# Neighbourhood attention of an encoder block: query products of 512 columns, and keys kept in token order

## The chip, the cores and the metric

The kernel runs on one core of a Trainium2 chip. The metric is the device time of one execution in microseconds (us); each kernel is run several times and the median is given. A profile is one more execution, recorded by the hardware profiler; its span runs from the first to the last instruction. Engines are named as the profile names them: PE (matrix products) with PEld (its weight loads), DVE (vector), ACT (scalar), POOL (GpSimd) and SP, which issues the DMAs.

## The reference, cut to what matters

One encoder block is computed for one sequence of 1024 tokens with 1024 features. After a modulated norm, one input projection gives queries, keys and values for two attentions, eight heads of 64 features each, and two gates. The change touches the second attention: the tokens stand on a grid of 16 rows and 64 columns, and each query attends to a window of 8 x 16 tokens that is clamped to the grid.

```python
q5 = q.reshape(B, rows, GRID_W, H, Dh)            # rows = 16, GRID_W = 64
row_start = jnp.clip(r - kh // 2, 0, rows - kh)   # kh = 8
col_start = jnp.clip(cq - NA_COLS // 2, 0, GRID_W - NA_COLS)   # NA_COLS = 16
s = jnp.einsum('brqhd,brakhd->bhrqak', q5, kr) * scale + bias[None]
s = jnp.where(col_mask[:, None, :], s, -jnp.inf)
p = jax.nn.softmax(s, axis=(-2, -1))
o = jnp.einsum('bhrqak,brakhd->brqhd', p, vr)
```

The first attention is a mixture of three dilated windows over the same sequence. Both outputs are projected, gated, summed, projected again and added to the residual; a ConvFFN (two large products with a depthwise convolution and a GELU between) and a final norm follow.

## The kernel before, in words

**Token order.** Everything is kept transposed, features on the 128 partitions and tokens along the free axis. The 1024 tokens stand in the order (r, t): position 256 r + t holds token 4 t + r. For the grid, t is 16 w + x, where w is the grid row and 4 x + r the grid column. So the order is (r, w, x): four residues, sixteen rows, sixteen groups of four columns. A half `hf` is the 512 positions with r = 2 hf and 2 hf + 1.

**Precision.** A product is made of three: each operand is split into a high part (rounded to fp32r) and a low part, and `product` (lines 78 to 85) issues high x high (L83), high x low (L84) and low x high (L85) for each of eight blocks of 128 features, into one PSUM bank of 512 columns. Weight tiles are loaded by SP (L64), rounded by ACT (L56), and POOL forms the low part (L60).

**Queries and keys of one pair of heads** (`qk_steps`, L284). For each of two halves a product goes into a bank `pj`; there are two such banks, `ps_g`, shared by queries, keys and gates. `q_half` (L291) empties the bank for each of the two heads: ACT writes the high part into `qs` (L305), DVE the difference (L306). `k_half` (L327) does the same with a factor 1/8: ACT L339, DVE L340, ACT L341, and POOL L342 copies the low part to the other 64 partitions.

**The neighbourhood branch (br = 1) before.** Its queries are wanted in the order (c, w, r, x'): c is one of four blocks of 16 columns, x' one of four groups in it, so that 128 neighbouring queries (one c, eight rows) form a block. `q_windows` (L308) therefore reads the moving operand `h` in that order, one residue at a time: for each of the eight blocks and three parts, two products of 256 columns (L315), 48 for a half instead of 24. The bank is then written to `qs` in runs of eight (L303 to L306). Its keys are stored in the order (w, x, r), so L339 to L342 write every fourth element of a half's share.

**The attention itself** (`attend_na`, L713). For each head, four blocks of columns `cb` and two row groups R: the score product (L735) takes 128 queries against twelve rows and n = 6 or 8 groups of columns, 288 or 384 keys, once with the high keys and once with the low ones; the keys of one row are one run of 24 or 32 elements. DVE adds the bias and takes the extreme (L739), ACT exponentiates (L741), DVE and POOL normalise (L746), PE transposes (L756), ACT and DVE split (L759, L760), PE multiplies with the values (L768), ACT and DVE add the two halves into the output tile (L774, L775), and SP writes it to `o_scr` (L776). The banks of the scores are two (`ps_l`).

**Values.** They are written to DRAM in token order and copied once per column block from DRAM to DRAM by 16 DMAs (`vb_chunks`, L382 to L387), into rows ordered like the keys: (w, x, r). `vb_load` (L539) loads them for each head.

**What sets the order.** The start (L389 to L537) and the gated branch products (L848 to L904) are written out by hand. Between them a scheduler orders the instructions of every engine by a timeline of its own: the loop at L790 issues, for eight pairs of heads (four dilated, four neighbourhood), the attention of pair n and then the queries and keys of pair n + 1 and one or two gates (`gate_tile`, L778). So products for the next pair fill PE while DVE and ACT work on scores. Gates evict through ACT L784. After the last gate the branch products need the last pair's output back from DRAM: `o_operands` (L822) loads it (L829), and ACT and DVE split it (L56, L60 into `o1hi`, `o1lo`). Then come the output projection and the ConvFFN (L906 on), again ordered by the scheduler.

Of the kernel before, what the change touches and what calls it, by code (L numbers as in the profile page):

```python
# [11 lines left out]
AF = mybir.ActivationFunctionType  # L12
OP = mybir.AluOpType
# [5 lines left out]
KT = 8  # L19
# [5 lines left out]
NA_T0 = (0, 2, 6, 10)  # L25
# [3 lines left out]
def hybrid_encoder(tc, xT, c, w_ada, small, w_in, p1_bias, p23_bias, na_bias, ln2_mult, ident, w_br, w_out,  # L29
                   w_up, w_down, out):  # L30
    nc = tc.nc
    act, dve, pool, pe, sp = nc.scalar, nc.vector, nc.gpsimd, nc.tensor, nc.sync
# [5 lines left out]
    def f(ap):  # L38
        return ap.bitcast(FT)
# [50 lines left out]
    h = {}  # L90
# [143 lines left out]
    vb_s = [v_scr[64 * sum(NA_NC[:cb]):64 * sum(NA_NC[:cb + 1])] for cb in range(4)]  # L234
# [49 lines left out]
    def qk_steps(br, pr, ws=None, ps=None):  # L284
        qt, kt = ((0, 4), (12, 16))[br]
        qs = [qkpool.tile([128, S], FR, name="qs") for _ in range(2)]
        ks = [qkpool.tile([128, S], FR, name="ks") for _ in range(2)]
        kl = [qkpool.tile([128, S], FR, name="kl") for _ in range(2)]
        qb = []

        def q_half(hf, w, p=None):  # L291
            cols = halves[hf]
            if p is None:
                p = ps_g.tile([128, 512], FT, name="pj")
                if br == 0:
                    product(p, w, lambda k: h[hf, k])
                else:
                    q_windows(p, w, hf)
            for i in range(2):
                a, b = slice(64 * i, 64 * i + 64), slice(64 - 64 * i, 128 - 64 * i)  # L300
                d, pp = qs[i][:, cols], p
                if br:
                    d = qs[i].rearrange("p (v r t) -> p v r t", v=64, r=4)[:, :, 2 * hf:2 * hf + 2]  # L303
                    pp = p.rearrange("p (r v t) -> p v r t", r=2, v=64)
                act.activation(d[a], pp[a], AF.Copy)  # L305
                dve.tensor_tensor(d[b], pp[a], f(d[a]), OP.subtract)  # L306

        def q_windows(p, w, hf):  # L308

            whi, wlo = w  # L310
            for k in range(KT):
                mhi, mlo = (t.rearrange("p (r w c t) -> p r c w t", r=2, w=16, c=4) for t in h[hf, k])
                for x, (ww, m) in enumerate(((whi, mhi), (whi, mlo), (wlo, mhi))):
                    for r in range(2):
                        pe.matmul(p[:, 256 * r:256 * r + 256], ww[:, k], m[:, r], start=k + x + r == 0,  # L315
                                  stop=k == KT - 1 and x == 2, skip_group_check=True)

        def q_blocks():
            for i in range(2):
                q = qkpool.tile([128, S], FR, name="qb", bufs=2)  # L320
                for r in range(4):
                    pool.tensor_scalar(q.rearrange("p (b r j) -> p r b j", b=8, r=4)[:, r],
                                       f(qs[i][:, 256 * r:256 * r + 256]).rearrange("p (b j) -> p b j", b=8), 1.0, None,
                                       OP.mult)
                qb.append(q)

        def k_half(hf, w, p=None):  # L327
            cols = halves[hf]
            if p is None:
                p = ps_g.tile([128, 512], FT, name="pj")  # L330
                product(p, w, lambda k: h[hf, k])
            for i in range(2):
                a, b = slice(64 * i, 64 * i + 64), slice(64 - 64 * i, 128 - 64 * i)
                kh, ll, pp = ks[i][:, cols], kl[i][:, cols], p
                if br:
                    kh, ll = (t.rearrange("p (w t r) -> p r w t", w=16, t=16)[:, 2 * hf:2 * hf + 2]
                              for t in (ks[i], kl[i]))
                    pp = p.rearrange("p (r w t) -> p r w t", r=2, w=16)
                act.activation(kh[a], pp[a], AF.Copy, scale=0.125)  # L339
                dve.scalar_tensor_tensor(ll[a], pp[a], 0.125, f(kh[a]), OP.mult, OP.subtract)  # L340
                act.activation(kh[b], pp[a], AF.Copy, scale=0.125)  # L341
                pool.tensor_scalar(ll[b], f(ll[a]), 1.0, None, OP.mult)  # L342

        if ws:
            for hf in range(2):
                yield
                if hf:
                    ps = [ps_g.tile([128, 512], FT, name="pj") for _ in range(2)]
                    for k in range(KT):
                        for p, w in zip(ps, ws):  # L350
                            product(p, w, lambda k: h[1, k], ks=[k])
                q_half(hf, ws[0], ps[0])
                k_half(hf, ws[1], ps[1])
            yield
            q_blocks()
        else:
            w = weights(qt + pr, pool)
            for hf in range(2):
                q_half(hf, w)
            if br == 0:  # L360
                q_blocks()
            w = weights(kt + pr, pool)
            for hf in range(2):
                k_half(hf, w)
        return qs, ks, kl, qb
# [16 lines left out]
    def vb_chunks():  # L382
        for cb in range(4):
            t0, n = NA_T0[cb], NA_NC[cb]
            for r in range(4):
                sp.dma_start(vb_s[cb].rearrange("(w t r) n -> r w t n", r=4, t=n)[r],
                             vb_c[256 * r:256 * r + 256].rearrange("(w t) n -> w t n", t=16)[:, t0:t0 + n])  # L387

    with tc.manual_schedule(engines={e.engine for e in (sp, act, dve, pool, pe)}):  # L389
        x = [x_load(0)]  # L390
# [34 lines left out]
        for q in range(4):  # L425
            ks = range(2 * q, 2 * q + 2)
# [76 lines left out]
        for n, (br, hv, st) in enumerate(v_steps[:19]):  # L503
# [17 lines left out]
            p = v_product(st, v_w[br, hv])  # L521
# [191 lines left out]
    def attend_na(pr, qk, work):  # L713
        qs, ks, kl, qb = qk
        oT = work.tile([128, S], FT, name="u1")
        for i in range(2):
            head = 2 * pr + i
            a = slice(64 * i, 64 * i + 64)
            kv, lv = (t.rearrange("p (w c) -> p w c", w=16) for t in (ks[i], kl[i]))
            st = work.tile([128, 2, 8], FT, name="stb")  # L720
            vv = v_tile(v_raw(vb_load, head), ((96, slice(0, 4)), (128, slice(4, 12)), (96, slice(12, 16))))
            col = 0
# [1 line left out]
            for cb in range(4):  # L724
                t0, n = NA_T0[cb], NA_NC[cb]
                kn = 48 * n
                bt = sm_pool.tile([128, 896], FT, name="bias", bufs=2)
                sp.dma_start(bt[:, :2 * kn], na_bias[head][:, col:col + 2 * kn])
                P = sm_pool.tile([128, 2, 384], FT, name="P", bufs=5)
                for R in range(2):  # L730
                    s = ps_l.tile([128, 512], FT, name="S")
                    d = s[:, :kn]
                    qc = slice(256 * cb + 128 * R, 256 * cb + 128 * R + 128)
                    for x_, t in enumerate((kv, lv)):
                        pe.matmul(d, qs[i][:, qc], t[:, 4 * R:4 * R + 12, 4 * t0:4 * t0 + 4 * n], start=x_ == 0,  # L735
                                  stop=x_ == 1)
                    e = 2 * cb + R
                    pp = P[:, R, :kn]
                    dve.tensor_tensor_reduce(pp, d, bt[:, kn * R:kn * R + kn], -1.0, BIG, OP.add, OP.min,  # L739
                                             st[:, 0, e:e + 1])  # L740
                    act.activation(pp, pp, AF.Exp, bias=st[:, 0, e:e + 1], scale=-1.0, accum_out=st[:, 1, e:e + 1])  # L741
                col += 2 * kn
                dve.reciprocal(st[:, 1, 2 * cb:2 * cb + 2], st[:, 1, 2 * cb:2 * cb + 2])  # L743
                for R in range(2):
                    pp = P[:, R, :kn]
                    (pool, dve)[R].tensor_scalar(pp, pp, st[:, 1, 2 * cb + R:2 * cb + R + 1], None, OP.mult)  # L746
                pn[cb] = P
            for pair in ((0, 3), (1, 2)):
                m = 16 * NA_NC[pair[0]]
# [13 lines left out]
                for y, cb in enumerate(pair):  # L763
                    jobs = ((1, t3[y], 128, 0, 256), (2, t3[2], 256 * y, 0, 256), (0, t3[y], 0, 0, 128),
                            (3, t3[y], 384, 128, 128))
                    for x_, (g, tt, c0, d0, n) in enumerate(jobs):
                        for t in tt:
                            pe.matmul(po[:, 256 * y + d0:256 * y + d0 + n], vv[:m, 4 * cb + g], t[:m, c0:c0 + n],  # L768
                                      start=x_ == 0 and t is tt[0], stop=x_ == 3 and t is tt[1],
                                      skip_group_check=True)  # L770
# [65 lines left out]
    with tc.tile_pool(name="gate", bufs=1, reuse_waits="tile") as work:  # L836
# [37 lines left out]
        for i in range(2 * KT):  # L874
            m, hf = divmod(i, 2)
            cols = halves[hf]
# [551 lines left out]
def _na_index():  # L1428
    parts = []
    p = np.arange(128)[:, None]  # L1430
    for cb in range(4):
        n = NA_NC[cb]
        for R in range(2):
            k = np.arange(48 * n)[None, :]
            qr, qc = 8 * R + p // 16, 16 * cb + 4 * (p % 4) + p // 4 % 4
            kr, kc = 4 * R + k // (4 * n), 4 * NA_T0[cb] + k % (4 * n)
            r0, c0 = np.clip(qr - 4, 0, 8), np.clip(qc - 8, 0, 48)
            ok = (kr >= r0) & (kr < r0 + 8) & (kc >= c0) & (kc < c0 + 16)
            idx = np.clip(kr - qr + 7, 0, 14) * 31 + np.clip(kc - qc, -15, 15) + 15
            parts.append(np.where(ok, idx, 15 * 31))  # L1440
    return np.concatenate(parts, axis=1)
# [58 lines left out]
```

## Time and profile before

| what | value |
|---|---|
| time, median of 3 runs | 1553.82 us |
| lowest and highest run | 1552.45 and 1553.98 us |
| span of the profiled execution | 1553.3 us, which lies between the lowest and the highest run |
| mean granted TensorE clock | 0.987 |
| instructions | 22335 |
| moved by DMA | 196.88 MB, mean 127 GB/s |

The profiled execution has no time of its own besides its span; the median of the timed runs stands 0.5 us above that span. The page gives for each engine its busy time and its share of the span. A matmul's duration on the page (some 280 ns for 256 columns, 390 ns for 512) is longer than the distance from one matmul's start to the next one's, because they are pipelined; what a product costs PE is read from starts. The branch named above runs from about 380 us (the first queries of a neighbourhood pair) to 684 us.

### The profile page before, as it was taken

How to read it: one execution, taken by the hardware profiler on the slowest of the kernel's cores; microseconds unless marked ns; L12 is line 12 of the kernel's file. 1: busy time of each engine (PE TensorE's matmuls, PEld its weight loads, DVE VectorE, ACT ScalarE, POOL GpSimd, SP SyncE). 2: the span in 40 equal slices, each digit the busy share in tenths (PEclk: the TensorE clock that was granted, in tenths of full speed). 3: DMA queues.
4: the chain of work that ended last, by engine and by line, in shares of the span. 5: the costliest groups of instructions: out<-in, count | busy, mean ns of one | idle time of the engine just before them, and what ended most of it. 6: DMA issues, size and time to landing. Idle time of an engine off the chain costs nothing.

```text
span 1553.3 us, 22335 instructions
## 1 busy us (share of the span) xinstructions
PE 1504.7 (97%) x8028; PEld 1291.5 (83%) x8028; DVE 1007.7 (65%) x1880; ACT 804.0 (52%) x1448; POOL 822.5 (53%) x652
## 2 busy tenths in 40 slices
PE   8998999999999999999999898999999998999998
PEld 7998988888898998878888777888888887878777
DVE  6785375665666665535615898766666667787765
ACT  4432475665866777543335454444444446575542
POOL 1043253544427666311256758776666665779721
PEclk9999999999999999999999999999999999999999
DMA  9467321222524443557734212222222224523313
GB/s 352 168 214 258 87 86 62 85 74 91 160 89 120 133 142 111 169 191 243 227 133 149 82 46 104 92 85 82 81 82 82 81 75 155 199 81 122 115 55 109
DMA packets 112374, 196.88 MB, mean 127 GB/s; under 512 B 39944, under 2 KB 57736, under 8 KB 112264
## 3 DMA queue, kind: packets, MB, share of 16 engines
q1 hardware_dynamic: 111992, 195.20, 38.1%
q8 instruction: 63, 1.03, 0.3%
q14 instruction: 47, 0.39, 0.1%
q10 hardware_dynamic: 272, 0.26, 0.1%
HBM read 158.73 MB, written 42.47 MB: 130 GB/s over the span
## 4 chain that ended last, share of the span: by engine, by line
PE 73%; DVE 8%; POOL 6%; DMA 5%; ACT 4%; issue 3%; SPq 1%; DVEq 0%; ACTq 0%; POOLq 0%
PE pj L83 11%; PE pj L84 11%; PE pj L85 10%; PE pj L963 8%; PE pj L965 8%; PE pj L964 8%; POOL wsl L60 2%; DMA wraw<-w_down 2%; PE pj L315 2%; PE O L768 2%; PE pv L243 2%; PE pv L245 1%; PE pv L244 1%; DVE big L1158 1%; PE T L756 1%
## 5 line engine op out<-in xcount | busy, mean ns | idle before, releaser
L60 POOL TENSOR_TENSOR wlo<-wraw,whi 128x512 fp32r<-128x512 f32 (+1 forms) x154 | 193.9, 1281 | 244.3 <-ACT whi L56 224.1
L83 PE MATMUL pj<-h,whi 128*128 128x512 f32 x448 | 179.2, 400 | 4.1 <-ACT ks L341 1.7
L84 PE MATMUL pj<-h,whi 128*128 128x512 f32 x448 | 177.9, 397 | 1.6 <-DVE h L208 1.6
L85 PE MATMUL pj<-h,wlo 128*128 128x512 f32 x448 | 176.9, 395 | 0.0
L60 POOL TENSOR_TENSOR wsl<-big,wsh 128x512 fp32r<-128x512 f32 (+1 forms) x90 | 123.8, 1397 | 51.8 <-ACT wsh L56 51.8
L56 ACT ACTIVATE whi<-wraw 128x1024 fp32r<-128x1024 f32 (+2 forms) x81 | 81.3, 1004 | 84.7 <-PE pj L84 36.3
L342 POOL TENSOR_SCALAR kl<-kl 64x512 fp32r<-64x512 f32 x32 | 63.8, 1995 | 99.2 <-DVE kl L340 97.9
L1158 DVE SCALAR_TENSOR_TENSOR big<-wc,sm,big 128x256 f32<-128x256 f32 (+1 forms) x132 | 103.0, 828 | 16.8 <-ACT big L1152 16.6
L83 PEld LDWEIGHTS pj<-h,whi 128*128 128x128 f32 x448 | 84.8, 189 | 20.3 <-ACT ks L341 2.5
L84 PEld LDWEIGHTS pj<-h,whi 128*128 128x128 f32 x448 | 84.8, 189 | 17.9 <-DVE h L208 3.1
L593 DVE CUSTOM_DVE_ANT_0 P<-S,bias 128x256 f32<-128x256 f32 x128 | 51.6, 420 | 73.6 <-PE S L640 47.0
L85 PEld LDWEIGHTS pj<-h,wlo 128*128 128x128 f32 x448 | 84.7, 189 | 15.6
L594 ACT ACTIVATE P<-P,st 128x256 f32<-128x256 f32 x128 | 64.2, 502 | 32.9 <-DVE st L593 32.3
L243 PE MATMUL pv<-vwh,h 128*128 128x256 f32 x256 | 74.7, 292 | 4.3 <-ACT vs L250 4.3
L60 POOL TENSOR_TENSOR wsl<-wraw,wsh 128x384 fp32r<-128x384 f32 (+1 forms) x46 | 54.7, 1212 | 44.5 <-ACT wsh L56 44.4
L1158 DVE SCALAR_TENSOR_TENSOR big<-pj,sm,big 128x512 f32<-128x512 f32 x132 | 67.1, 563 | 16.4 <-ACT big L1152 16.4
L1152 ACT ACTIVATE big<-wc,sm 128x512 f32<-128x512 f32 x44 | 35.8, 815 | 74.4 <-DVE wc L976 42.8
L550 POOL TENSOR_TENSOR vv<-vv 96x256 fp32r<-96x256 f32 (+2 forms) x32 | 41.1, 1292 | 62.7 <-ACT vv L549 42.8
L245 PE MATMUL pv<-vwh,h 128*128 128x256 f32 x256 | 73.7, 288 | 0.0
L244 PE MATMUL pv<-vwl,h 128*128 128x256 f32 x256 | 73.7, 288 | 0.0
L746 POOL TENSOR_SCALAR P<-P,stb 128x288 f32<-128x288 f32 (+1 forms) x32 | 39.4, 1233 | 47.9 <-DVE stb L743 38.9
L56 ACT ACTIVATE wsh<-big 128x1024 fp32r<-128x1024 f32 (+1 forms) x45 | 44.7, 998 | 38.2 <-POOL big L928 22.5
(380 smaller groups left out, 4885.1 us busy)
## 6 DMA issues: line engine op xcount, KB each, us to landing
wraw<-w_in SPq DMA_DIRECT2D x36, 512.0 KB
wada<-w_ada SPq DMA_DIRECT2D x31, 512.0 KB
big<-w_up SPq DMA_DIRECT2D x22, 512.0 KB
wraw<-w_up SPq DMA_DIRECT2D x22, 512.0 KB
as<-big SPq DMA_DIRECT2D x22, 512.0 KB
big<-as SPq DMA_DIRECT2D x22, 512.0 KB
wraw<-w_down SPq DMA_DIRECT2D x24, 384.0 KB
gs<-gs SPq DMA_DIRECT2D x32, 256.0 KB
```

The costliest lines, as they stand in the source:

```text
L56: act.activation(hi, raw, AF.Copy)
L60: lo_eng.tensor_tensor(lo[:, i:i + step], raw[:, i:i + step], f(hi)[:, i:i + step], OP.subtract)
L83: pe.matmul(psum, whi[:, k0 + k], mhi, start=k == 0, stop=False)
L84: pe.matmul(psum, whi[:, k0 + k], mlo, start=False, stop=False)
L85: pe.matmul(psum, wlo[:, k0 + k], mhi, start=False, stop=k == n - 1)
L243: pe.matmul(p, hhi, hi[:, k], start=fresh and k == 0, stop=False, skip_group_check=True)
L244: pe.matmul(p, hhi, lo[:, k], start=False, stop=False, skip_group_check=True)
L245: pe.matmul(p, hlo, hi[:, k], start=False, stop=k == KT - 1, skip_group_check=True)
L963: pe.matmul(psum, whi[:, k], bhi, start=j < 4 and k == 0, stop=False, skip_group_check=True)
L964: pe.matmul(psum, whi[:, k], blo, start=False, stop=False, skip_group_check=True)
L965: pe.matmul(psum, wlo[:, k], bhi, start=False, stop=k == n - 1, skip_group_check=True)
L1158: dve.scalar_tensor_tensor(y[:, dst], src, wt, y[:, dst], OP.mult, OP.add)
```

## The change

The query product of the neighbourhood branch is issued by `product`, 512 columns at a time. It reads `h` as (w, x, r): four neighbouring groups x of one residue, then the other residue of the half. The bank is written to `qs` in the same places as before, with another rearrangement. The keys stay in token order (r, w, x): the writes of L339 to L342 are plain. The score product's moving operand picks, for each of twelve rows and each of four residues, the n groups of columns it needs, so a run is 6 or 8 elements where it was 24 or 32. The bias (built on the host, `_na_index`) and the values (`vb_chunks`) take the same key order: row, residue, group. The DMAs from DRAM to DRAM then write n rows of 2 KB in one run.

```diff
             if br:
-                d = qs[i].rearrange("p (v r t) -> p v r t", v=64, r=4)[:, :, 2 * hf:2 * hf + 2]
-                pp = p.rearrange("p (r v t) -> p v r t", r=2, v=64)
+                d = qs[i].rearrange("p (c w x) -> p c w x", c=4, w=16)[:, :, :, 8 * hf:8 * hf + 8]
+                pp = p.rearrange("p (w c x) -> p c w x", w=16, c=4)
             act.activation(d[a], pp[a], AF.Copy)
             dve.tensor_tensor(d[b], pp[a], f(d[a]), OP.subtract)
...
         def q_windows(p, w, hf):
-            whi, wlo = w
-            for k in range(KT):
-                mhi, mlo = (t.rearrange("p (r w c t) -> p r c w t", r=2, w=16, c=4) for t in h[hf, k])
-                for x, (ww, m) in enumerate(((whi, mhi), (whi, mlo), (wlo, mhi))):
-                    for r in range(2):
-                        pe.matmul(p[:, 256 * r:256 * r + 256], ww[:, k], m[:, r], start=k + x + r == 0,
-                                  stop=k == KT - 1 and x == 2, skip_group_check=True)
+            product(p, w, lambda k: [t.rearrange("p (r v t) -> p v r t", r=2, v=64) for t in h[hf, k]])
...
-                kh, ll, pp = ks[i][:, cols], kl[i][:, cols], p
-                if br:
-                    kh, ll = (t.rearrange("p (w t r) -> p r w t", w=16, t=16)[:, 2 * hf:2 * hf + 2]
-                              for t in (ks[i], kl[i]))
-                    pp = p.rearrange("p (r w t) -> p r w t", r=2, w=16)
-                act.activation(kh[a], pp[a], AF.Copy, scale=0.125)
-                dve.scalar_tensor_tensor(ll[a], pp[a], 0.125, f(kh[a]), OP.mult, OP.subtract)
-                act.activation(kh[b], pp[a], AF.Copy, scale=0.125)
+                kh, ll = ks[i][:, cols], kl[i][:, cols]
+                act.activation(kh[a], p[a], AF.Copy, scale=0.125)
+                dve.scalar_tensor_tensor(ll[a], p[a], 0.125, f(kh[a]), OP.mult, OP.subtract)
+                act.activation(kh[b], p[a], AF.Copy, scale=0.125)
                 pool.tensor_scalar(ll[b], f(ll[a]), 1.0, None, OP.mult)
...
-                sp.dma_start(vb_s[cb].rearrange("(w t r) n -> r w t n", r=4, t=n)[r],
+                sp.dma_start(vb_s[cb].rearrange("(w r t) n -> r w t n", r=4, t=n)[r],
                              vb_c[256 * r:256 * r + 256].rearrange("(w t) n -> w t n", t=16)[:, t0:t0 + n])
...
-            kv, lv = (t.rearrange("p (w c) -> p w c", w=16) for t in (ks[i], kl[i]))
+            kv, lv = (t.rearrange("p (r w t) -> p w r t", r=4, w=16) for t in (ks[i], kl[i]))
...
-                        pe.matmul(d, qs[i][:, qc], t[:, 4 * R:4 * R + 12, 4 * t0:4 * t0 + 4 * n], start=x_ == 0,
-                                  stop=x_ == 1)
+                        pe.matmul(d, qs[i][:, qc], t[:, 4 * R:4 * R + 12, :, t0:t0 + n], start=x_ == 0, stop=x_ == 1)
...
-            kr, kc = 4 * R + k // (4 * n), 4 * NA_T0[cb] + k % (4 * n)
+            kr, kc = 4 * R + k // (4 * n), 4 * (NA_T0[cb] + k % n) + k // n % 4
```

Built, the changed kernel has the same instructions on every engine but PE, which has 192 matmuls fewer: the 384 of L315 are gone, and L83, L84 and L85 have 64 more each. Up to the first of them (380 us) the order on each engine is as before. From there to the branch products, and in a short stretch at the start of the ConvFFN, the scheduler puts the same instructions in another order.

## The prediction

> **What bounds the kernel now.** I read the page's busy times first, then the busy times by stretch, then who waited for whom in the branch's own stretch, 380 to 684 us.
>
> ```profile
> PE 1504.7 (97%) x8028; PEld 1291.5 (83%) x8028; DVE 1007.7 (65%) x1880; ACT 804.0 (52%) x1448; POOL 822.5 (53%) x652
> ```
> ```profile
> 380.00:455.00 75.00, 71.31 (x474) 64.59 (x473) 49.77 (x141) 52.19 (x118) 32.68 (x24) 1.00 0.40 122
> 455.00:605.00 150.00, 148.18 (x985) 135.12 (x984) 101.63 (x257) 109.61 (x230) 96.93 (x72) 1.00 0.44 128
> 605.00:684.00 79.00, 79.00 (x434) 68.15 (x432) 36.84 (x90) 45.35 (x93) 28.87 (x24) 1.00 0.52 169
> 900.00:980.00 80.00, 74.85 (x307) 59.70 (x307) 69.65 (x87) 36.38 (x47) 59.53 (x42) 0.95 0.22 79
> ```
> ```profile
> PE S L609 <- DVE st L593: 2.4, 2, 2.1
> PE pj L83 <- ACT ks L341: 1.7, 2, 1.3
> PE pj L83 <- DVE qs L306: 0.8, 2, 0.6
> PE S L735 <- DVE stb L739: 0.6, 1, 0.6
> ```
>
> The columns of the second fence are stretch, length, then busy time of PE, PEld, DVE, ACT, POOL. PE bounds the branch: it is idle for 75.00 - 71.31 = 3.7 us, 1.8 us and nothing. All its waits there sum to 5.5 us (third fence: total, times, longest). So an edit gains only if it makes PE's own products cheaper, or takes one of these waits; DVE, ACT and POOL have room. The start of the ConvFFN (fourth stretch, DVE busy 69.65 of 80) is the only later place whose order changes.
>
> **The change part by part.**
>
> *Query products: 384 of 256 columns become 192 of 512.* Their price is the distance of starts, in an undisturbed run of each kind.
>
> ```profile
> 558.24 0.62 PE L315 MATMUL pj<-h,whi 128*128 128x256 f32 x4
> ...
> 560.79 0.39 PE L315 MATMUL pj<-h,wlo 128*128 128x256 f32 x2
> 561.02 0.34 PE L735 MATMUL S<-ks,qs 128*128 128x384 f32 x1
> ...
> 671.02 0.39 PE L83 MATMUL pj<-h,whi 128*128 128x512 f32 x1
> ...
> 673.51 0.28 PE L768 MATMUL O<-th,vv 128*128 128x256 f32 x1
> ```
>
> 24 products of 256 columns (4 + 2, four times) stand between 558.24 and 561.02: 2.78 us, 116 ns each. 11 of 512 stand between 671.02 and 673.51: 2.49 us, 226 ns each, 2.72 us for twelve. So a half query product costs half as much, and the halved count of instructions and weight loads brings only 0.06 us for 24: over 384, 16 x 0.06 = **-1.0 us**. The new operand has runs of four elements too (four groups, two residues, 64 times), and the 116 ns were measured on runs of four: no penalty is taken.
>
> *Score products: the same 128, with runs of 6 or 8 instead of 24 or 32.*
>
> ```profile
> 478.80 0.34 PE L735 MATMUL S<-ks,qs 128*128 128x384 f32 x1
> ...
> 479.51 0.40 PE L85 MATMUL pj<-h,wlo 128*128 128x512 f32 x1
> ```
> ```profile
> 470.99 0.29 PE L735 MATMUL S<-ks,qs 128*128 128x288 f32 x1
> 471.12 0.30 PE L735 MATMUL S<-kl,qs 128*128 128x288 f32 x1
> 471.25 0.50 PE L315 MATMUL pj<-h,whi 128*128 128x256 f32 x3
> ```
>
> Four of 384 keys take 0.71 us (178 ns each), two of 288 take 0.26 us (130 ns): 64 x 0.178 + 64 x 0.130 = 19.7 us in all. The trace has no run of 6 or 8. The nearest row is L315's runs of four, which cost 116 ns for 256 columns, no more per column than L735's long runs (178 / 384 x 256 = 119 ns). I take **0**. On one side a gain is excluded by the column rate, on the other the bound is the doubling that ACT shows below for single elements: +19.7 us.
>
> [...]
>
> *Key writes.* The same four operations serve dilated pairs (plain writes, before 400 us) and neighbourhood pairs (every fourth element, after); one row for each, for L339, L340 and L342.
>
> ```profile
> 0.00:400.00 400.00, 9.43 (x16) 0.98 0.44 147
> 400.00:610.00 210.00, 17.27 (x16) 1.00 0.42 125
> ```
> ```profile
> 0.00:400.00 400.00, 10.99 (x16) 0.98 0.44 147
> 400.00:610.00 210.00, 17.44 (x16) 1.00 0.42 125
> ```
> ```profile
> 0.00:400.00 400.00, 24.09 (x16) 0.98 0.44 147
> 400.00:610.00 210.00, 39.75 (x16) 1.00 0.42 125
> ```
>
> ACT falls from 1.08 to 0.59 us, DVE from 1.09 to 0.69, POOL from 2.48 to 1.51; L341 is of L339's kind. That is 15.7 us of ACT, 6.5 of DVE and 15.7 of POOL, all beside PE. What reaches PE is the wait of L83 for the bank that L341 empties last: 1.7 us in two places. The chain L339, L340, L341 for a head shrinks from 3.25 to 1.87 us, so both waits (1.3 us the longer) go: **-1.7 us**; 0 if DVE is late with L340, -2.3 if half of L306's and L735's 1.4 us goes as well.
>
> [...]
>
> *Query writes.* They read and write runs of eight where they read runs of four; ACT and DVE cost the same for dilated and neighbourhood queries (L306's row below has one mean for both kinds): 0, from both sides.
>
> *Values.* 16 copies keep their place in SP's queue, with longer runs and the same bytes.
>
> ```profile
> 412.50:416.00 3.50, 3.50 (x26) 3.20 (x24) 1.40 (x4) 2.13 (x4) 2.49 (x1) 1.00 0.00 1
> ...
> 428.00 1.95 SPq L543 DMA_DIRECT2D vv<-v x4
> ```
>
> All queues are empty from 412.5 us (DMA share 0.00), and the first load of a copied value is issued at 428.0: 15.5 us of cover. 0, also if the copies took half as long or some 15 us more.
>
> *The order.* PE meets its waits in another place, and this costs more than any edit. At the first one (387.7 us, L609 for L593, 2.1 us) DVE is at the dilated epilogue. The built order puts 19 query products behind the first score product, which fills that wait; but behind them come ten score products and twelve transposes without a filler, where before some 50 short query products were strewn among them. I take **0**, between -2 and +2.
>
> The second place is the first neighbourhood head. After the last dilated output the changed order has on PE 14 transposes (L704), 16 score products (L735), 4 transposes (L756) and one L768 before the next key product, which waits for the last L306 of the query bank. Before, 50 query products stood among them.
>
> ```profile
> L739 DVE CUSTOM_DVE_ANT_0 P<-S,bias x64: 439/502/559, 461.9 to 643.9; 128x288 f32<-128x288 f32 x32, 128x384 f32<-128x384 f32 x32
> L756 PE MATMUL T<-idt,P x192: 269/272/299, 471.8 to 668.3; 128*96 128x128 f32 x96, 128*128 128x128 f32 x96
> ```
> ```profile
> 469.94 0.68 DVE L706 TENSOR_TENSOR u<-u,T 128x512 f32<-128x512 f32 x1
> ...
> 472.17 0.43 DVE L746 TENSOR_SCALAR P<-P,stb 128x384 f32<-128x384 f32 x1
> ```
> ```profile
> L306 DVE TENSOR_TENSOR qs<-pj,qs 64x512 fp32r<-64x512 f32 x32 | 22.0, 689 | 13.8 <-ACT qs L305 13.0
> L564 DVE TENSOR_TENSOR u<-O,u 64x512 f32<-64x512 f32 x32 | 21.8, 683 | 18.0 <-ACT u L563 17.6
> ```
>
> DVE must do in that time: one L564 (0.68), three L739 of 384 (0.55), two of 288 (0.45), four L706 (0.68), two reciprocals (0.17, an estimate), one L746 (0.43), one L306 (0.69): 0.68 + 1.65 + 0.90 + 2.72 + 0.34 + 0.43 + 0.69 = 7.4 us. PE has 8 x 0.178 + 8 x 0.130 + 18 transposes at some 0.11 (an estimate below their 0.27 of latency) + 0.12 = 4.6 us. So PE waits 2.8 to 3.4 us; the last two rows of the waits (1.4 us) go with it: **+2.0 us**, between 0 and +3.4.
>
> *The end of the branch.*
>
> ```profile
> 675.41 0.27 PE L768 MATMUL O<-tl,vv 128*128 128x128 f32 x1
> ...
> 685.36 0.39 PE L85 MATMUL pj<-h,wlo 128*128 128x512 f32 x1
> ...
> 686.86 1.37 ACT L56 ACTIVATE o1hi<-oraw 128x512 fp32r<-128x512 f32 x2 [3.25 <-DMA oraw<-ob]
> ...
> 688.13 0.58 ACT L784 ACTIVATE gs<-pj 128x512 f32<-128x512 f32 x1
> ...
> 688.76 0.50 PE L83 MATMUL pj<-o0hi,whi 128*128 128x512 f32 x1 [3.02 <-ACT gs L784]
> ...
> 691.59 0.63 PE L83 MATMUL pj<-o0hi,whi 128*128 128x512 f32 x1
> ```
>
> From the last L768 to the branch products 13.3 us pass; 38 gate products fill 8.6 of them, and the last gate's eviction stands on ACT behind splits that wait for the reload. The changed order has only 16 gate products there, but that eviction ahead of the splits. So nine or more branch products can go before the reload is in; the last pair's still wait for it. 22 products earlier, some 22 later: **-0.2 us**, between -2 (if no half-speed stretch, the 0.63 us products, follows) and +1.
>
> *ConvFFN start:* the same instructions in another order, DVE bound: 0, between -1.5 and +1.5.
>
> **Sum:** -1.0 + 0 - 1.7 + 0 + 2.0 - 0.2 + 0 = -0.9 us on the span: 1553.3 - 0.9 = 1552.4. The median stands 0.5 above the span: 1552.9 us.
>
> **The rivals.** 0.2% is 3.1 us, about what a measurement of this kernel can tell from no change: "same" is 1550.7 to 1556.9.
>
> *PE's waits go.* The idler ACT, POOL and DVE answer faster everywhere, so the 5.5 us of waits and the half-speed stretch after the reload go: -1.0 - 5.5 = -6.5, 1547.3 us. For it: 38 us of side work go. Against: only 1.7 us of the waits name a key write.
>
> *The bunching costs (slower).* Queries done in fewer, longer products are done earlier, so fewer fillers are left between scores, and PE runs at DVE's pace at the head of the branch, twice (+2.0 more at the first place), and a wait of over 3 us there brings a half-speed stretch of 3.4 us (1.7 us lost), as the one at 685 us did; with 2 us more in the ConvFFN the sum is -0.9 + 2.0 + 1.7 + 2.0 = +4.8: 1558.6 us. It decides from waits of 4 us over those of now. For it: the order as built. Against: 150 of 304 us of the branch are far from DVE's limit.
>
> *Short runs slow the score products:* at the upper bound +19.7 - 0.9, 1572.6 us.
>
> **How the numbers follow.** The forecast 0.5, waits go 0.2, bunching 0.25, short runs 0.05. The forecast's own range is 1549.5 to 1556.5. The range 1546.5 to 1559 takes in most of the second and third cases. Faster 0.25 (0.2 and a tenth of the forecast), same 0.45, slower 0.30.
>
> **What would show it.** Right: L83's 512 columns at some 226 ns in the query products; L339, L341 at 0.59, L340 at 0.69, L342 at 1.5 us; L735 at 178 and 130 ns; no wait of L83 for the key writes; a wait of about 3 us at the first neighbourhood head. Wrong: longer distances of L735 or of the query products, a lower clock between 380 and 500 us, or a branch that ends more than 3 us from 684 us on.

## The result and the profile after

The kernel after takes 1561.79 us (median of 5 runs, 1559.74 to 1562.34) against 1553.98 us for the kernel before beside it (5 runs, 1552.45 to 1555.66): ratio **1.0049, interval 1.0037 to 1.0062**, some 7.8 us slower. The forecast was 1552.9 us, no change; the time lies above its range too.

The page's busy times and the busy times by stretch of the kernel after (PE, PEld, DVE, ACT, POOL, then the granted clock, the DMA share and GB/s):

```profile
PE 1513.4 (97%) x7836; PEld 1283.1 (82%) x7836; DVE 996.7 (64%) x1880; ACT 787.8 (51%) x1448; POOL 805.9 (52%) x652
```
```profile
380.00:455.00 75.00, 74.53 (x423) 63.33 (x422) 45.23 (x140) 48.07 (x117) 27.50 (x22) 1.00 0.40 127
455.00:605.00 150.00, 147.52 (x781) 122.69 (x780) 86.43 (x237) 91.25 (x210) 79.67 (x67) 0.99 0.39 113
605.00:684.00 79.00, 79.00 (x433) 67.53 (x431) 36.85 (x93) 44.12 (x97) 30.30 (x26) 1.00 0.51 153
```

The instructions went as planned: 192 products fewer, DVE, ACT and POOL 11 to 17 us less busy. Yet PE is busy 8.7 us longer. Where does that time lie? Look at one instruction ahead of the change and one behind the branch, in the kernel before and then in the kernel after (timeline of PE: start, duration, line):

```profile
355.04 0.28 PE L609 MATMUL S<-ks,qs 128*128 128x256 f32 x1
...
723.18 0.39 PE L83 MATMUL pj<-o0hi,whi 128*128 128x512 f32 x1
...
871.98 0.48 PE L963 MATMUL pj<-B11hi,whi 128*128 128x512 f32 x1
...
986.38 0.39 PE L963 MATMUL pj<-B11hi,whi 128*128 128x512 f32 x1
```
```profile
351.94 0.28 PE L599 MATMUL S<-ks,qs 128*128 128x256 f32 x1
...
730.33 0.39 PE L83 MATMUL pj<-o0hi,whi 128*128 128x512 f32 x1
...
879.24 0.49 PE L952 MATMUL pj<-B11hi,whi 128*128 128x512 f32 x1
...
990.95 0.39 PE L952 MATMUL pj<-B11hi,whi 128*128 128x512 f32 x1
```

These are the same products (lines stand ten or eleven lower after). Between the first two rows before takes 368.14 us and after 378.39: **the branch costs 10.25 us more.** Between the last two before takes 114.40 and after 111.71: the start of the ConvFFN costs 2.7 us less. Together 7.6 us, as the medians say. The spans (1557.6 and 1553.3) differ by less only because the profiled execution of after came to the branch 3.1 us sooner, over code that is the same; up to there before ran at half the granted clock (0.50) in three stretches of 3.4 us more than after, at 52, 130 and 277 us.

What is dearer in the branch shows in the starts of the products. First score products of 384 columns, then of 288:

```profile
491.13 0.43 PE L725 MATMUL S<-ks,qs 128*128 128x384 f32 x1
491.38 0.43 PE L725 MATMUL S<-kl,qs 128*128 128x384 f32 x1
491.64 0.29 PE L757 MATMUL O<-th,vv 96*128 96x256 f32 x1
...
531.56 0.34 PE L725 MATMUL S<-ks,qs 128*128 128x288 f32 x1
...
532.22 0.40 PE L83 MATMUL pj<-h,whi 128*128 128x512 f32 x1
```

Two of 384 take 0.51 us (before: four in 0.71); the four of 288 between 531.56 and 532.22 take 0.66, 165 ns each (before 130). Medians over 64 products of each shape, here and below taken from all starts of the timeline: **264 ns against 179, and 172 against 134**. Now 19 query products of 512 columns without anything between them:

```profile
388.92 0.41 PE L85 MATMUL pj<-h,wlo 128*128 128x512 f32 x1
...
393.42 0.41 PE L85 MATMUL pj<-h,wlo 128*128 128x512 f32 x1
393.67 0.28 PE L599 MATMUL S<-ks,qs 128*128 128x256 f32 x1
```

19 in 4.75 us: 250 ns each, where a plain product of 512 takes 226 and two old ones 2 x 115. The median of all 192 is **253 ns**. A distance above 1.08 times the median is taken to hold a wait; counted as 1.08 times the median, the totals are:

| products | before, us | after, us | difference |
|---|---|---|---|
| query | 44.2 | 48.4 | +4.2 |
| score, 384 columns | 11.6 | 17.0 | +5.4 |
| score, 288 columns | 8.6 | 11.0 | +2.4 |

That is +12.0 us, more than the whole loss. Of the other large groups only the plain product's median moved, from 227 to 230 ns. The waits of PE after, from 355 to 705 us:

```profile
PE pj L83 <- ACT gs L773: 2.4, 1, 2.4
PE S L725 <- DVE stb L728: 2.2, 3, 1.3
PE O L659 <- DVE tl L589: 0.2, 1, 0.2
PE S L629 <- DVE st L583: 0.2, 1, 0.2
PE T L745 <- DVE u L696: 0.2, 1, 0.2
```

They sum to 5.2 us; before it was 5.5 in the prediction's list and 3.0 for L83 <- L784 at 685 us, 8.5. The two waits for a key write (L341, now L331) are gone. Its four operations cost what the plain ones cost; ACT's L329, DVE's L330 and POOL's L332 in the branch:

```profile
400.00:610.00 210.00, 9.41 (x16) 0.99 0.39 116
```
```profile
400.00:610.00 210.00, 11.01 (x16) 0.99 0.39 116
```
```profile
400.00:610.00 210.00, 24.02 (x16) 0.99 0.39 116
```

So 0.59, 0.69 and 1.50 us each.

### The profile page after: what moved, and what is told of

Its sections match the earlier page's. It is cut to its first block, busy times and chain, and to the rows that moved or that the text cites. A ratio compares the mean times of both kernels' runs of the same rounds, so it can differ in the third digit from the quotient of the medians.

```text
span 1557.6 us, 21948 instructions
## 1 busy us (share of the span) xinstructions
PE 1513.4 (97%) x7836; PEld 1283.1 (82%) x7836; DVE 996.7 (64%) x1880; ACT 787.8 (51%) x1448; POOL 805.9 (52%) x652
## 5 line engine op out<-in xcount | busy, mean ns | idle before, releaser
L83 PE MATMUL pj<-h,whi 128*128 128x512 f32 x512 | 205.8, 402 | 2.3 <-ACT h L206 2.2
L84 PE MATMUL pj<-h,whi 128*128 128x512 f32 x512 | 205.0, 400 | 2.1 <-DVE h L208 2.1
L85 PE MATMUL pj<-h,wlo 128*128 128x512 f32 x512 | 204.2, 399 | 0.0
L60 POOL TENSOR_TENSOR wsl<-big,wsh 128x512 fp32r<-128x512 f32 (+1 forms) x90 | 123.7, 1396 | 48.4 <-ACT wsh L56 48.4
L1147 DVE SCALAR_TENSOR_TENSOR big<-wc,sm,big 128x256 f32<-128x256 f32 (+1 forms) x132 | 106.4, 854 | 16.0 <-ACT big L1141 15.9
L84 PEld LDWEIGHTS pj<-h,whi 128*128 128x128 f32 x512 | 97.0, 189 | 21.7 <-DVE h L208 3.4
L83 PEld LDWEIGHTS pj<-h,whi 128*128 128x128 f32 x512 | 97.0, 189 | 21.7 <-ACT h L206 2.8
L85 PEld LDWEIGHTS pj<-h,wlo 128*128 128x128 f32 x512 | 96.9, 189 | 18.6
L583 DVE CUSTOM_DVE_ANT_0 P<-S,bias 128x256 f32<-128x256 f32 x128 | 51.8, 420 | 75.5 <-PE S L630 43.0
L332 POOL TENSOR_SCALAR kl<-kl 64x512 fp32r<-64x512 f32 x32 | 48.1, 1503 | 93.9 <-DVE kl L330 90.0
L735 POOL TENSOR_SCALAR P<-P,stb 128x288 f32<-128x288 f32 (+1 forms) x32 | 39.2, 1226 | 63.7 <-DVE stb L732 54.7
L56 ACT ACTIVATE wsh<-big 128x1024 fp32r<-128x1024 f32 (+1 forms) x45 | 44.7, 998 | 48.4 <-POOL big L917 35.8
```

Source lines behind the costliest of these rows:

```text
L56: act.activation(hi, raw, AF.Copy)
L60: lo_eng.tensor_tensor(lo[:, i:i + step], raw[:, i:i + step], f(hi)[:, i:i + step], OP.subtract)
L83: pe.matmul(psum, whi[:, k0 + k], mhi, start=k == 0, stop=False)
L84: pe.matmul(psum, whi[:, k0 + k], mlo, start=False, stop=False)
L85: pe.matmul(psum, wlo[:, k0 + k], mhi, start=False, stop=k == n - 1)
L1147: dve.scalar_tensor_tensor(y[:, dst], src, wt, y[:, dst], OP.mult, OP.add)
```

## The experiments

**Each half of the change alone.** The first kernel takes the query product and its write into the kernel before; the second takes the keys, their bias and values.

```diff
-            whi, wlo = w
-            for k in range(KT):
...
-                        pe.matmul(p[:, 256 * r:256 * r + 256], ww[:, k], m[:, r], start=k + x + r == 0,
+            product(p, w, lambda k: [t.rearrange("p (r v t) -> p v r t", r=2, v=64) for t in h[hf, k]])
```

> The kernel before with the query products alone changed (512 columns, its write to match; keys, bias and values as before). If the query products cost what they cost in the kernel after (254 ns for 512 columns against two of 114 to 116), they add 192 x 0.254 - 384 x 0.115 = 4.6 us, and the waits among the short products (3 us) may go: a median of 1555.5 to 1558.5, score products at 178 and 132 ns. Rival (the slow score products and the order carry all, the query products cost only beside them): 226 ns a product and a median of 1552.5 to 1554.

Measured: 1558.38 us, ratio 1.0020 (1.0007 to 1.0033). The query products take 253 ns, the score products 180 and 133. The rival falls: the new query product is dear without the new keys.

> The kernel before with the keys alone in token order (bias, values and score operand to match; query products as before). Theory: score products at 264 and 172 ns against 178 and 132, 64 x 0.086 + 64 x 0.040 = 8.1 us more, less up to 1.7 us of waits for key writes: a median of 1560 to 1562.5. Rival (the order, not the operand, makes the kernel after slow): score products near 178 and 132 ns when filled between other products, and a median within 2 us of 1554.

Measured: 1561.44 us, ratio 1.0039 (1.0024 to 1.0053). The score products take 263 and 172 ns between short query products as well; the rival falls. Both halves cost, 3 and 6 us by their ratios. They need not add up to the whole exactly, since each kernel also has an order of its own: in the second PE waits 5.5 us for the last gate's eviction, before 3.0. An order can move this kernel by more (the last experiments below), so it is the distances of starts that show the price, and the times agree with them.

**Is it the run's length, its jump or where it starts?** After the change a run of 8 keys starts at group 2 or 6 of its row, 8 bytes off a 16-byte line (a line is here four elements that begin at a multiple of 16 bytes; it is the author's unit, which the starts below bear out: 183 to 187 ns from elements 0, 4 and 8, 260 to 267 from 1, 2 and 3). The next kernel changes only where a run starts; the order of every engine stays.

```diff
-                        pe.matmul(d, qs[i][:, qc], t[:, 4 * R:4 * R + 12, :, t0:t0 + n], start=x_ == 0, stop=x_ == 1)
+                        pe.matmul(d, qs[i][:, qc], t[:, 4 * R:4 * R + 12, :, (3, 4, 6, 10)[cb]:][..., :n], start=x_ == 0, stop=x_ == 1)
```

> The kernel after, order unchanged; the score product reads other keys than the reference's: each 16-token row is read from token 3, 4, 6, 10 for the four column blocks instead of 0, 2, 6, 10 (blocks of 6, 8, 8, 6 keys). Nothing else moves. Theory L (a product's operand costs some 1.77 ns for each 16-byte line that its runs touch, 0.442 ns a column for whole lines): block 0 now touches 3 lines a run instead of 2 and goes from 172 to some 255 to 265 ns; block 1 touches 2 instead of 3 and falls from 264 to some 171 to 180 ns; blocks 2 and 3 stay at 264 and 172. Rival J (each jump of 1024 bytes between runs has its price, whatever the start): no block moves, 172, 264, 264, 172. Rival R (price by the number of columns and runs alone): the same as J.

Timeline of PE, block 1 (starts at group 4), then block 2 of the same head (starts at 6, as in after):

```profile
486.15 0.35 PE L725 MATMUL S<-ks,qs 128*128 128x384 f32 x1
...
486.89 0.40 PE L85 MATMUL pj<-h,wlo 128*128 128x512 f32 x1
...
495.32 0.43 PE L725 MATMUL S<-ks,qs 128*128 128x384 f32 x1
495.57 0.44 PE L725 MATMUL S<-kl,qs 128*128 128x384 f32 x1
495.83 0.39 PE L745 MATMUL T<-idt,P 128*128 128x128 f32 x2
```

Four products in 0.74 us, 185 ns each, against two in 0.51. So runs of 8 with the same jumps are nearly as cheap as the old runs of 32 (179 ns) once they start on a line: rivals J and R fall. Theory L is half right: block 0 did not go to 255 ns but stayed near 180.

The next kernel gives each head its own start, and lets two heads read all twelve rows of one residue before the next, with jumps of 64 bytes.

```diff
-            kv, lv = (t.rearrange("p (r w t) -> p w r t", r=4, w=16) for t in (ks[i], kl[i]))
+            o, s0, s1 = (("w r", (0, 10), (2, 6)), ("w r", (0, 8), (0, 8)), ("w r", (4, 4), (4, 4)), ...)[head]; kv, lv = ...
...
+                        pe.matmul(d, qs[i][:, qc], t[:, 4 * R:4 * R + 12, :, (s0[0], s1[0], s1[1], s0[1])[cb]:][..., :n].rearrange(f"p w r t -> p {o} t"), ...)
```

> The kernel after, order unchanged; each of the eight heads reads its score operand from other tokens of the rows, so the scores are not the reference's (head 0 is as in the kernel after). Runs of 8 start at token 2, 6 (head 0), 0, 8 (head 1), 4 (2), 1 (3), 3 (4), 2 (5), 2, 6 (6), 4, 8 (7); runs of 6 at 0, 10; 0, 8; 4; 1; 3; 2; 0, 10; 4, 8. Heads 6 and 7 take the 12 rows of one residue before the next residue, so the jumps are 64 bytes instead of 1024. Theory A (a run of 8 pays when it doesn't start on a 16-byte line): 187 ns in heads 1, 2, 7, some 264 in 0, 3, 4, 5, 6; runs of 6 stay within 156 to 190 in all heads. Rival J (the 1024-byte jump makes the misaligned start dear): 187 in 6 as well as in 7, the rest as A. Rival G (32-byte granules): 187 in head 1 alone, 264 in heads 2 and 7.

Timeline of PE: head 7 (two products, start 4, jumps of 64 bytes), then head 6 (four, start 2, the same jumps):

```profile
641.23 0.34 PE L725 MATMUL S<-ks,qs 128*128 128x384 f32 x1
...
641.58 0.39 PE L83 MATMUL pj<-h,whi 128*128 128x512 f32 x1
```
```profile
618.47 0.42 PE L725 MATMUL S<-ks,qs 128*128 128x384 f32 x1
...
619.46 0.40 PE L83 MATMUL pj<-h,whi 128*128 128x512 f32 x1
```

Two in 0.35 us and four in 0.99. Medians of eight products of 384: starts 0 and 8: 183 ns; 4: 187; 1: 260; 3: 267; 2: 261; with jumps of 64 bytes, 2 and 6: 250; 4 and 8: 174.5. (Head 0 lies among PE's waits for DVE at the head of the branch and isn't read.) Theory A holds in the seven others; J and G fall. The 1024-byte jump costs 9 to 12 ns a product, the start off the line 73 to 84. Runs of 6 take 167 to 180 ns wherever they start.

The same question for the long runs and for runs of 4, in the kernel before:

```diff
-                        pe.matmul(d, qs[i][:, qc], t[:, 4 * R:4 * R + 12, 4 * t0:4 * t0 + 4 * n], start=x_ == 0,
-                                  stop=x_ == 1)
+                        o, y, m = (0, 2, 1, 3, 0, 2, 0, 2)[head], (0, 0, 0, 0, 16, 16, 8, 8)[head], (0, 0, 0, 0, n, n, 4, 4)[head]
+                        pe.matmul(d, qs[i][:, qc], t[:, 4 * R:4 * R + 12].rearrange("p w (x y) -> p w x y", y=y)[:, :, :n * 4 // m, o:o + m] if y else t[:, 4 * R:4 * R + 12, 4 * t0 + (o, o, o, -o)[cb]:][:, :, :4 * n], start=x_ == 0, stop=x_ == 1)
```

> The kernel before, order unchanged; the score product reads other keys in each of the eight heads, so the scores are not the reference's. Heads 0 to 3: the long runs of before (32 and 24 elements), begun 0, 2, 1 and 3 elements off a 16-byte line. Heads 4, 5: runs of 8 (6 in the product of 288) 64 bytes apart, begun 0 and 2 elements off. Heads 6, 7: runs of 4, 32 bytes apart, begun 0 and 2 off. Theory A1 (an operand is read four columns at a time; a start off the line makes each such read touch two lines): 384 columns cost 178 in heads 0, 4, 6 and some 250 to 265 in heads 1, 2, 3, 5, 7, long runs too. Rival A2 (only the ends of a run pay): 12 runs instead of 48 pay a quarter of 77 ns, some 197 in heads 1 to 3, 255 in head 5, more than 255 in head 7 (96 runs).

Timeline of PE: four products of long runs begun two elements off (head 1), three of runs of 4 on the line (head 6), two of runs of 4 off it (head 7):

```profile
475.40 0.36 PE L736 MATMUL S<-ks,qs 128*128 128x384 f32 x1
...
476.18 0.39 PE L85 MATMUL pj<-h,wlo 128*128 128x512 f32 x1
...
607.34 0.34 PE L736 MATMUL S<-kl,qs 128*128 128x384 f32 x1
...
607.86 0.39 PE L84 MATMUL pj<-h,whi 128*128 128x512 f32 x1
...
629.57 0.50 PE L736 MATMUL S<-ks,qs 128*128 128x384 f32 x1
629.89 0.53 PE L736 MATMUL S<-kl,qs 128*128 128x384 f32 x1
630.24 0.42 PE L83 MATMUL pj<-h,whi 128*128 128x512 f32 x1
```

195 ns (four in 0.78), 173 (three in 0.52) and 335 (two in 0.67). Rival A2 holds and A1 falls: twelve long runs off the line pay 15 ns together (195 against 180), not the 72 to 87 that A1 has. Put beside the number of 16-byte lines that the runs touch, each at 226 / 128 = 1.77 ns (the plain product of 512):

| operand | lines | lines x 1.77 | measured, ns |
|---|---|---|---|
| 12 runs of 32, on and off the line | 96, 108 | 170, 191 | 180, 195 |
| 12 runs of 24, on and off | 72, 84 | 127, 149 | 134, 160 |
| 48 runs of 8, 64 bytes apart, on and off | 96, 144 | 170, 255 | 174, 252 |
| 96 runs of 4, on and off | 96, 192 | 170, 340 | 174, 341 |
| 48 runs of 6 from an even group | 96 | 170 | 163 to 180 |

So, within 11 ns, **an operand of these shapes costs by the lines its runs touch**, and the score products of after stand within 9 ns of the count, 264 for 255 and 172 for 170: a run of 8 from group 2 touches three lines (2, 4, 2), and a run of 6 two, of which one is half used, where 24 touched six full ones. One shape doesn't fit: runs of 6 from group 3 touch three lines (1, 4, 1) and should cost 255 ns, but cost 180.

**The query product.** Its runs of 4 all start on a line and touch 128 lines, as the plain product does, so the count gives 226 and not 253. The next two kernels read `h` in another order in each of the eight blocks of the contraction.

```diff
-            product(p, w, lambda k: [t.rearrange("p (r v t) -> p v r t", r=2, v=64) for t in h[hf, k]])
+            product(p, w, lambda k: [t.rearrange("p (r v t) -> p v r t", r=(2, 4, 8, 32, 2, 2, 2, 1)[k], t=(4, 4, 4, 4, 8, 2, 1, 4)[k]) for t in h[hf, k]])
```

> The kernel after, order unchanged; the query product of a neighbourhood pair reads its 512 tokens in another order in each of the eight slices of the contraction (so the queries are not the reference's). Slices 0 to 3: runs of 4 tokens with jumps of 1024, 512, 256 and 64 bytes; slices 4, 5, 6: jumps of 1024 bytes with runs of 8, 2 and 1 tokens; slice 7: one plain run of 512. Theory L alone (16-byte lines touched at 1.77 ns): 226 ns in slices 0 to 4 and 7, 453 in slice 5, 905 in slice 6; slice 0 was 254 in the kernel after, so L needs a second price. Rival J (0.22 ns for each jump, of any length): 254 in slices 0 to 3, 240 in 4, 283 in 5, 339 in 6, 226 in 7. L with a price on the 1024-byte distance only (two lines 1024 bytes apart collide): 254 in slice 0, 226 in 1, 2, 3 and 7, some 240 in 4, over 453 in 5 and 905 in 6.

Timeline of PE; each row is the first of the three products of a slice, slices 2 to 7:

```profile
389.22 0.45 PE L83 MATMUL pj<-h,whi 128*128 128x512 f32 x1
...
390.06 0.38 PE L83 MATMUL pj<-h,whi 128*128 128x512 f32 x1
...
390.73 0.40 PE L83 MATMUL pj<-h,whi 128*128 128x512 f32 x1
...
391.45 0.51 PE L83 MATMUL pj<-h,whi 128*128 128x512 f32 x1
...
392.45 0.39 PE L83 MATMUL pj<-h,whi 128*128 128x512 f32 x1
...
393.11 0.39 PE L83 MATMUL pj<-h,whi 128*128 128x512 f32 x1
```

A third of each distance is one product: 280 ns for runs of 4 with jumps of 256 bytes, 223 with 64, 240 for runs of 8 with 1024, 333 for runs of 2, 220 for single elements. The second kernel has r=(16, 16, 8, 4, 2, 8, 32, 16) and t=(4, 8, 8, 8, 16, 16, 2, 1):

> As the earlier run with eight operand orders of the query product, in the kernel after, with eight other orders, all begun on a 16-byte line. Slices 0 to 7: runs of 4 with jumps of 128 bytes; of 8 with 128, 256 and 512; of 16 with 1024 and 256; of 2 with 64; single elements with 128. Theory D (a jump costs nothing up to 64 bytes and 0.2 to 0.4 ns beyond, more for 256 than for 1024, whatever the run): slice 0 at 254 to 280 (127 jumps), 1 to 3 at 240 to 253 (63), 4 and 5 at 233 to 240 (31), 6 at 228. Rival P (the price goes by the distance as a power of two under 1024 and not by the count of jumps): slices 2 and 5 as dear as the earlier run's runs of 4 at 256 bytes, 278.

Medians of 24 products, in ns (512 columns):

| run | jump 64 bytes | 128 | 256 | 512 | 1024 |
|---|---|---|---|---|---|
| 16 elements | | | 237 | | 240 |
| 8 | | 232 | 258 | 231 | 243 |
| 4 | **228** | 245 | 278 | 265 | **254** |
| 2 | 431 | | | | 331 |
| 1 | | 434 | | | 216 |

The two bold cells are the old query product's jump and the new one's: on top of the lines, a jump beyond 64 bytes costs a run of 4 17 to 50 ns a product. None of the theories gives the whole table. The single price per jump (J) falls at 228, a price at 1024 bytes alone at 278 and 265, theory D at 431 and 231, P at 237. Why 256 bytes is worst, and how runs shorter than a line are read, stays open.

**Does the start off the line matter for the time?** The keys are stored two elements further, so that runs of 8 start on a line. The space for it comes from one small tile, `st` of the dilated branch, which moves to another pool; that changes the order of the instructions from about 160 us on.

```diff
-        ks = [qkpool.tile([128, S], FR, name="ks") for _ in range(2)]
-        kl = [qkpool.tile([128, S], FR, name="kl") for _ in range(2)]
+        ks = [qkpool.tile([128, S + 2], FR, name="ks")[:, 2 * br:2 * br + S] for _ in range(2)]
+        kl = [qkpool.tile([128, S + 2], FR, name="kl")[:, 2 * br:2 * br + S] for _ in range(2)]
...
-        st = sm_pool.tile([128, 2, 4, 8], FT, name="st")
+        st = work.tile([128, 2, 4, 8], FT, name="st")
```

> The kernel after with the keys of the neighbourhood pairs stored two elements (8 bytes) further, so that the runs of 8 start on a 16-byte line; the reference's result is kept. The order is not quite that of the kernel after. Theory A: the 64 products of 384 columns fall from 264 to some 187 ns, 4.9 us less: a median of 1556 to 1558. Rival (the start costs nothing in the time, because PE waits for DVE instead at the head of the branch): 1560 to 1562.

Measured: 1549.29 us, ratio 0.9973 (0.9961 to 0.9984), far more than forecast.

> The kernel of the run with the keys alone in token order, with the same two elements of padding: old query products of 256 columns, score products on whole lines. Theory A: 64 x 0.077 = 4.9 us less than that run's 1561.4, a median of 1555.5 to 1557.5, within 0.2% of the kernel before; left over are 64 x 0.040 us of the products of 288 columns, which have whole lines neither way. Rival as above: 1560 to 1562.

Measured: 1544.43 us, ratio 0.9938 (0.9922 to 0.9955). Both gain more than the start can give, so the move of `st` had to be taken apart from it. Three kernels have that one line alone, on the kernel before, the kernel after and the kernel with the keys alone:

> The kernel before with one small tile, the dilated branch's st (its minima and sums), taken from the pool of the branch's working tiles instead of the softmax pool, as both padded kernels need for their space; the result is kept, the order changes from the modulation sums on. If the move of st is what makes the padded kernels fast, it is worth some 5 to 7 us here too: a median of 1547 to 1549. If it is worth nothing by itself: 1552.5 to 1555.

Measured: **1543.14 us, ratio 0.9930** (0.9917 to 0.9944), below both forecasts and the lowest median of all (the padded kernel with the keys alone, ratio 0.9938, lies within its interval): the move gains 0.7% by itself.

> The kernel after with st moved in the same way and no padding: every engine's order is that of the padded kernel after, so the two differ in the first byte of the keys alone. Theory A (a run of 8 that starts off a 16-byte line pays some 75 ns a product): 64 x 0.077 = 4.9 us over the padded kernel's 1549.3, a median of 1553 to 1555.5. Rival (the move of st did it all): 1548.5 to 1550.5.

Measured: 1554.37 us, ratio 1.0013 (1.0002 to 1.0024), as theory A had it. This kernel and its padded twin issue the same instructions in the same order, so what lies between them is the start's alone: 5.1 us by the medians and 6 by the ratios (the two were not timed beside each other). The branch in the two (timeline of PE, without and with padding) takes 346.92 us between these rows, and 342.35, a difference of 4.6 us where the theory has 4.9:

```profile
349.93 0.27 PE L606 MATMUL T<-idt,P 128*128 128x128 f32 x1
...
696.85 0.39 PE L83 MATMUL pj<-o0hi,whi 128*128 128x512 f32 x1
```
```profile
349.97 0.27 PE L606 MATMUL T<-idt,P 128*128 128x128 f32 x1
...
692.32 0.40 PE L83 MATMUL pj<-o0hi,whi 128*128 128x512 f32 x1
```

> The kernel with the keys alone in token order and st moved, without padding: the order of the padded one of the two. Theory A: 4.9 us over its 1544.4, a median of 1548 to 1550.5. Rival (the move of st did it all, or PE's waits take the gain up): 1543.5 to 1546.

Measured: 1546.93 us, ratio 0.9959 (0.9945 to 0.9972). This lies between the two forecasts: 2.5 us over its padded twin instead of 4.9. In the branch of the two profiles the distance is 4.2 us (340.70 against 336.52), and the two intervals allow it; the medians alone would not show it.

The three kernels with `st` moved were timed beside each other, and they show the change in another order: 1543.14 us without it, 1546.93 with the keys alone, 1554.37 with both halves. The whole change costs 11.2 us there, near the 12.0 that the products cost; its halves, 3.8 and 7.4, divide otherwise than above, since each kernel has its own order.

Of the fastest kernel PE's longest waits from 195 to 705 us:

```profile
PE S L609 <- DVE st L593: 1.9, 2, 1.6
PE pj L83 <- ACT ks L341: 1.6, 2, 1.2
PE pj L83 <- ACT gs L784: 1.0, 1, 1.0
```

In all they sum to 6.6 us, against 11.0 in the kernel before over the same stretch; L83 <- L784 fell from 3.0 to 1.0. The kernel before also has two stretches of 3.4 us at half the granted clock there, at 277 and 690 us, and this one is granted 1.00 from 245 to 710 us. The gain is one of order. Which of the reordered instructions brings it was not tried.

## Why the prediction was wrong

The step that failed is the price of the two new operands, "no penalty is taken" and "I take **0**". Point by point:

- **Query products, -1.0 us: wrong, +4.2.** The argument was that the new operand has runs of four too and that L315's runs of four cost nothing. They did, but with jumps of 64 bytes; the new ones jump 1024. Runs of 4 at 64 bytes cost 228 ns for 512 columns and at 1024 bytes 254. Here a row stood for an operand only where run, start and jump were all the same.
- **Score products, 0: wrong, +7.8**, inside the bound of 19.7. The same row was taken for runs of 6 and 8, and the rival "short runs" got a chance of 0.05. It was right in part: the runs show a price not on the shortness but on the lines touched, 144 instead of 96 (264 ns against 179) and 96 instead of 72 (172 against 134).
- **The bound of 19.7 us:** the doubling it was taken from is 1.83 times by ACT's own rows (17.27 us against 9.43), and 1.59 and 1.65 by those of DVE and POOL. For the operands of PE, the runs of 8 that start on an even element off the line have at least two elements in each of their three lines and cost 264 ns, against 187 on the line; 48 pieces that begin on a line, 64 bytes apart, cost 174 ns, no more than 12 long ones (180).
- **Key writes, -1.7 us: right.** Durations as forecast, and both waits are gone. L306's 0.8 us went as well.
- **Values and query writes, 0: right.** No wait names them.
- **Order, first place, 0:** 2.4 us of waits for L593 became 0.4 (L659 for L589, L629 for L583), a gain of 2.0, at the edge of its range.
- **Order, second place, +2.0:** the burst stands where it was put, and PE waits there 2.2 + 0.2 us where before it waited 0.6 (L735 for L739). The working gave 7.4 - 4.6 - 1.4 = 1.4 us; the 2.0 needs 3.4 us of waiting, for which no row was given. With it stands what the rival "bunching" named, half the clock for 3.4 us, the first row (after); before, such a stretch stood behind the reload at 690 us, the second row. That it takes a wait of over 3 us is not shown: the first stands behind two waits for L728 of 1.9 us in all, the longer 1.3, the second behind one of 3.0:

```profile
474.50:477.90 3.40, 3.40 (x10) 2.52 (x9) 3.31 (x5) 0.30 (x2) 2.70 (x3) 0.51 0.81 264
```
```profile
690.20:693.50 3.30, 3.30 (x9) 2.52 (x9) 0.32 (x1) 0.40 (x1) 2.51 (x2) 0.50 0.97 346
```

- **End of the branch, -0.2:** the wait fell from 3.0 to 2.4 us, and no stretch at half clock follows it (the granted clock is 1.00 from 684 to 880 us). The two stretches cancel.
- **ConvFFN start, 0:** -2.7 us, outside the bound of 1.5. The instructions are the same in another order. PE's waits of over 0.15 us sum to 9.5 us there, before to 11.2, and both kernels spend 10.2 us at half the clock; the cause was not tried further.

The sum of the branch: +4.2 + 7.8 - 3.3 (named waits, 5.2 for 8.5) = +8.7 of the measured 10.25. The other 1.5 us lie in longer distances beside waits and are not assigned. The rival "bunching" came nearest to the time (1558.6) by luck: what it named cost little here.

## What to carry to other kernels

Before an operand of the matrix engine is cut into pieces, count the 16-byte lines that its pieces touch: here each cost some 1.77 ns, used in full or not, and moving the whole tile by 8 bytes won 5.1 us in the kernel after and 2.5 with the keys alone (`st` moved in both). The count is no full price: jumps of 128 to 1024 bytes added 17 to 50 ns to a product of runs of 4, and runs shorter than a line (216 to 434 ns) and one of the runs of 6 (180 ns, 255 by the count) did not follow it. In this kernel long pieces written with a stride by an engine that has room were worth more than short pieces read by the engine that bounds it (the keys in token order cost 3.8 us, 1546.93 against 1543.14). A price from the trace held here for an operand with the same run, start and jump, and not with another jump (254 ns against 228) or start (264 against 187); where one of them differs, take it as unknown and keep its upper bound in the forecast. And where a scheduler builds the order, run the neutral edit too: moving one tile of 256 bytes a partition won 0.7% here, more than the change itself moved.

## What the runs showed of the hardware that was not expected

- Runs of 4 cost more with jumps of 256 bytes (278 ns for 512 columns) than with 512 (265) or 1024 (254), and nothing with 64 (228 against 226 for the plain product).
- Single elements taken by turns from two places 1024 bytes apart cost 216 ns, less than the plain product's 226, though a count of line changes would make it 905; single elements 128 bytes apart cost 434.
- Runs of 6 from group 3 of a row cost 180 ns, though they touch three lines; runs of 8 that touch three, with the same jumps, have medians of 260 to 267.
